# Layer 0: four of nine late output tiles as split products, and an earlier schedule for the modulation weights

## The chip, the cores and the metric

The kernel runs on one core of a Trainium2 chip. The metric is the device time of one execution in microseconds. TensorE (PE) multiplies, PEld is its loading of weights, VectorE (DVE) and ScalarE (ACT) work element by element, GpSimd (POOL) helps with a few additions, and SyncE (SP) issues nearly all transfers from HBM, in one queue and in the order of the program.

## The reference

Two layers of an encoder on 256 tokens of 2048 features, in float32. In each layer:

```
mod = silu(c) @ w_ada + b_ada            # six vectors of 2048: sh1, sc1, g1, sh2, sc2, g2
u = x*(1+sc1) + sh1;  proj = u @ w_in    # three head groups A (4), B (6), C (6 heads)
y = concat(rms_norm(A), rms_norm(B), rms_norm(C))
x = layer_norm(alpha*x + (1+g1) * (y @ w_o))
u = x*(1+sc2) + sh2;  h = silu(u@w_g) * (u@w_u)
x = layer_norm(alpha*x + (1+g2) * (h @ w_down))
```

## The kernel before, in words

Activations lie feature by feature: a tile is 128 features by 256 tokens, so 2048 features are 16 tiles (`KT`), and one output tile sums 16 products of a 128x128 weight with such a tile.

A product is made in one of two ways. **In float32** (`gemm_f32`, L277 to L283): each of the 16 products is one call, which stands in the trace as two matmul rows; the weights come as two transfers of 512 KB straight into one `hi` and one `lo` buffer (`wload_f32`), with no work on ACT or DVE. **Split** (`gemm_one`, `gemm_t`): a 1 MB transfer goes into a `raw` buffer; ACT rounds it to the high half (L254), DVE subtracts to get the low half (L255), both in two pieces of 1024 columns; then `gemm_one` runs three matmuls of 256 columns per product (high x high, high x low, low x high: L314 to L316). There are four `raw`, four `hi` and four `lo` buffers, taken in turn. The normalised head outputs are kept in both forms: `Yf` in float32, `Y` as high and low halves.

The modulation `mod` is made by DVE beside everything else. `ada(n)` takes the next of a list of 192 pieces: a 1 MB transfer of `w_ada` into a `raw` buffer (L205), and a multiply-and-sum on DVE (L207) at the lowest scheduling priority. Two things call it. `pace(us)` is called at each weight load (5.2 us' worth for 2048 columns) and each head (3.0) and adds `rate * us` to a credit; each whole unit of credit issues one piece. `need(l, part, k)` issues at once whatever is still missing of that part. The list runs, for layer 0: parts 1 and 0 (32 pieces, done with the first products), part 2 (16), parts 4 and 3 (32, the feed-forward's modulation), part 5 (16); then layer 1. `RATE[0][0]` is the rate from the end of the first input products to the late output tiles.

In layer 0 the order is: input products; norms of the latent vectors; head group A, then B, then C, each woven with products that fill TensorE (in C the first ten products of output tiles 0 to 6, split, from seven loads of `w_o`); the last six products of tiles 0 to 6; then the loop over the 16 output tiles in which tiles 7 to 15 are made whole (the nine late tiles). Each tile goes into the residual on DVE (L582) and its sums for the norm (L594, L597, L598). Tile 15 and the sums close the stage; the layer norm and the gate/up products follow, whose first tiles are a split stream of the `gemm_one` kind. In the loop, all `need` of part 2 is met; at tile 12 the missing pieces of parts 4 and 3 are issued and the rate is set to zero.

Of the kernel before, what the change touches and what calls it, by code (L numbers as in the profile page):

```python
# [21 lines left out]
KT = D // P  # L22
# [24 lines left out]
HO, KC = 7, 10  # L47
# [44 lines left out]
T2K, T1K, RAWB, HIB = 28, 31, 4, 4  # L92

DEFER = 4
RATE = ((0.24, 0.135, 0.135), (0.04, 0.05, 0.05))
NPOOL = 4


# [9 lines left out]
def tile_encoder(ctx: ExitStack, tc: tile.TileContext, xT, cB, w_ada, vecs, rpb, sink, consts,  # L108
# [24 lines left out]
    def pg(name):  # L133
        return ps.tile([P, 512], F32, tag="g", bufs=4, name=name)
# [80 lines left out]
    def need(l, part, k=KT - 1):  # L215
        g = ada_group(l, part)
        k += g - 1 - k % g
        while (l, part, k) in ada_pending:
            ada(1)
# [21 lines left out]
    def wload(src, cols, splits, gates=(), lo_eng=None):  # L241
        uid[0] += 1
        u = uid[0]
        pace(5.2 * cols / 2048)
        raw = wp.tile([P, 2048], F32, tag="raw", bufs=RAWB, name=f"raw{u}")
        sy.dma_start(out=raw[:, :cols], in_=src)
        res = []
        c0 = 0
        for i, n in enumerate(splits):
            hi = wp.tile([P, 1024], F32R, tag="hi", bufs=HIB, name=f"hi{u}_{i}")  # L250
            lo = wp.tile([P, 1024], F32R, tag="lo", bufs=HIB, name=f"lo{u}_{i}")
            eng = lo_eng[i] if lo_eng else ve
            with after(*gates):
                ac.activation(out=hi[:, :n], in_=raw[:, c0:c0 + n], func=AF.Copy)  # L254
                eng.tensor_tensor(out=lo[:, :n], in0=raw[:, c0:c0 + n], in1=hi[:, :n].bitcast(F32), op=ALU.subtract)  # L255
            res.append((c0, n, hi, lo))
            c0 += n

        def get(c, n):
            for s0, m, hi, lo in res:  # L260
                if s0 <= c and c + n <= s0 + m:
                    return hi[:, c - s0:c - s0 + n], lo[:, c - s0:c - s0 + n]
            raise AssertionError
        return get

    def wload_f32(src):

        uid[0] += 1
        pace(5.2)
        res = []  # L270
        for i, tag in enumerate(("hi", "lo")):
            w = wp.tile([P, 1024], F32, tag=tag, bufs=HIB, name=f"wf{uid[0]}_{i}")
            sy.dma_start(out=w, in_=src[:, i * 1024:(i + 1) * 1024])
            res.append(w)
        return res

    def gemm_f32(acc, w, X, kts, between=None):  # L277
        for i, k in enumerate(kts):
            if between and i == len(kts) - 4:
                between()  # L280
            m_ = pe.matmul(acc[:, :S], lhsT=w[i // 8][:, i % 8 * P:(i % 8 + 1) * P], rhs=X[k][:], start=(i == 0),  # L281
                           stop=(i == len(kts) - 1))
        last_mm[0] = raw_ins(m_)  # L283

    def gemm_t(acc, get, c0, X, kts):

        n = len(kts)
        for run in (range(n),):
            for i in run:
                pe.matmul(acc[:], lhsT=get(c0 + i * P, P)[0], rhs=X[kts[i]][:], start=(i == 0), stop=False)  # L290
            for i in run:
                last_mm[0] = raw_ins(pe.matmul(acc[:, :S], lhsT=get(c0 + i * P, P)[1], rhs=X[kts[i]][:, :S],  # L292
                                               start=False, stop=(i == n - 1)))

    def gemm_last(acc, get, X, kts, between=None):

        ops = []
        for i, k in enumerate(kts):
            h, lo = get(i * P, P)
            ops += [(h, X[k][:, :S]), (h, X[k][:, S:]), (lo, X[k][:, :S])]  # L300
        for i, (w, x) in enumerate(ops):
            if between and i == len(ops) - 12:
                between()
            m_ = pe.matmul(acc[:, :S], lhsT=w, rhs=x, start=(i == 0), stop=(i == len(ops) - 1))
        last_mm[0] = raw_ins(m_)

    def gemm_one(acc, get, c0, X, kts):

        for i, k in enumerate(kts):
            h, lo = get(c0 + i * P, P)  # L310
            mm_one(acc, h, lo, X[k], i == 0, i == len(kts) - 1)

    def mm_one(acc, h, lo, x, first, end, **kw):
        m_ = pe.matmul(acc[:, :S], lhsT=h, rhs=x[:, :S], start=first, stop=False, **kw)  # L314
        pe.matmul(acc[:, :S], lhsT=h, rhs=x[:, S:], start=False, stop=False, **kw)
        last_mm[0] = raw_ins(pe.matmul(acc[:, :S], lhsT=lo, rhs=x[:, :S], start=False, stop=end, **kw))  # L316
        return raw_ins(m_)
# [262 lines left out]
    def residual(l, acc, n, gate_, s1, s2, final, name, one=False):  # L580
        if final and (n == KT - 1 or one):
            ve.scalar_tensor_tensor(out=ax[:, n], in0=acc[:, :S], scalar=gate_, in1=ax[:, n], op0=ALU.mult, op1=ALU.add)  # L582
        else:
            t = tmp(f"rt_{name}")
            ac.activation(out=t, in_=acc[:, S:], func=AF.Identity, scale=gate_)  # L585
            (ve if final and n == KT - 2 else po).tensor_tensor(out=ax[:, n], in0=ax[:, n], in1=t, op=ALU.add)  # L586
            ve.scalar_tensor_tensor(out=ax[:, n], in0=acc[:, :S], scalar=gate_, in1=ax[:, n], op0=ALU.mult, op1=ALU.add)
        if final:
            if n == 0:
                ac.activation(out=s1, in_=ax[:, n], func=AF.Copy)  # L590
                ac.activation(out=s2, in_=ax[:, n], func=AF.Square)
            else:
                q = tmp(f"rq_{name}")
                i1 = ac.activation(out=q, in_=ax[:, n], func=AF.Square)  # L594
                if n == KT - 1:
                    return q
                (ve if one or n == KT - 2 else po).tensor_tensor(out=s1, in0=s1, in1=ax[:, n], op=ALU.add)  # L597
                d1 = ve.tensor_tensor(out=s2, in0=s2, in1=q, op=ALU.add)  # L598
                return raw_ins(d1), raw_ins(i1)
        return None  # L600

    allk = list(range(KT))
# [42 lines left out]
    def head_block(src, made, gates, name):  # L645
        accs = [pg(f"{name}_{i}") for i in range(4)] + [pa("s", 2, f"{name}_{i}") for i in range(4, HB)]
        st = Stream(_stream_head(), src, name, gates)
        for n, k in st.seq:
            st.load()
            if k not in X:  # L650
                X[k] = made(k)
            st.mm(accs[n], n, k, k == 0, k == KT - 1)
        return accs
# [3 lines left out]
    for l in range(L):  # L657
# [94 lines left out]
        if l == 0:  # L752
# [14 lines left out]
            def first_half(j):  # L767
                n = ROT[j]
                half = rot[:, j % 2 * S:(j % 2 + 1) * S]
                take(st_in.tile(n, 0, HK, half), dst[n][0], dst[n][1])  # L770
# [8 lines left out]
            first_half(HK)  # L779
            credit[1] = RATE[l][0]  # L780
            for n in RES[8:] + RES[:8]:
# [4 lines left out]
        else:  # L786
            sy.dma_start(out=nba, in_=rpb[l])
            X = {}
            accs = head_block(w_in[l], made, gates, f"in{l}")
            credit[1] = RATE[l][0]  # L790
            for n, acc in zip(HEAD1, accs):
# [7 lines left out]
        Y, Yf = [None] * KT, [None] * KT  # L799
# [150 lines left out]

        for n in range(KT):
            need(l, 2, KT - 1 if l else n)
            if n == KT - 4:
                need(l, 3, KT - 1 if l else KT - 1 - DEFER // 2)
                credit[1] = 0.0
            if n < HO:
                acc = oacc[n]
            else:
                acc = pg(f"o{l}_{n}")
                if l == 0:  # L960
                    gemm_f32(acc, wload_f32(w_o[l, n]), Yf, allk, sums_in if n == KT - 1 else None)
                else:
                    get = wload(w_o[l, n], 2048, (1024, 1024))
                    if n == KT - 1:
                        gemm_last(acc, get, Y, allk, sums_in)
                    else:
                        gemm_t(acc, get, 0, Y, allk)
            r_ = residual(l, acc, n, mods[l, 2][:, n:n + 1], s1, s2, True, f"o{l}_{n}", l == 0)
            if n == KT - 2:
                lastr = r_  # L970
# [26 lines left out]
        for g in range(FFG):  # L997
            credit[1] = RATE[l][1 if g == 0 else 2]
            H = []
            for j in range(GSZ):  # L1000
                f = g * GSZ + j
                hs = []
                for w in range(2):
# [5 lines left out]
                    if 2 * f + w < HB and l:  # L1009
                        acc = head[2 * f + w]  # L1010
                    else:
                        get = wload(w_gu[l, 2 * f + w], 2048, (1024, 1024))
                        acc = pg(f"gu{l}_{f}_{w}")
# [16 lines left out]
            c1 = (GSZ + 1) // 2  # L1030
            credit[1] = RATE[l][2]
            if g == FFG - 1:
# [5 lines left out]
            for n in range(KT):  # L1038
# [8 lines left out]
                get = wload(w_dn[l, g, n], GSZ * P, (c1 * P, (GSZ - c1) * P))  # L1047
                acc = pg(f"dn{l}_{g}_{n}")
# [137 lines left out]
```

## Time and profile before

| | |
|---|---|
| median of 3 runs | 2286.91 us (2285.03 to 2287.71) |
| the profiled execution | 2284.07 us |
| its span, first to last instruction | 2282.3 us |
| PE, PEld, DVE, ACT, POOL busy | 97%, 85%, 72%, 51%, 9% |
| mean rate of transfers over the span | 259 GB/s |

The late output tiles of layer 0 run from 360.4 to 424 us of the span, the three head groups from about 201 to 360 us. A group of the page gives busy time, the mean duration of one instruction, and the idle time of its engine just before; the chain of waits is followed back from the last instruction.

### The profile page before, as it was taken

The numbers are of one execution on the slowest core, as the hardware profiler recorded it, in microseconds if no ns is written. First come the engines' busy times: TensorE is split into PE (matmuls) and PEld (weight loads), VectorE is DVE, ScalarE is ACT, GpSimd is POOL, SyncE is SP. The second block draws the span as 40 slices with busy tenths as digits, with TensorE's granted clock in tenths as the row PEclk, the third lists the DMA queues.
The fourth block names the chain that finished last, engine by engine and source line by source line (L and its number), as shares of the span: only waits on it lengthen the run. The fifth ranks groups of instructions, "written<-read, shape, count | busy, mean of one in ns | idle before, by whom it ended". The sixth has DMA issues, their size and how long they took to land.

```text
span 2282.3 us, 32742 instructions
## 1 busy us (share of the span) xinstructions
PE 2224.7 (97%) x12670; PEld 1946.2 (85%) x12670; DVE 1654.6 (72%) x2340; ACT 1157.0 (51%) x1955; POOL 196.3 (9%) x169
## 2 busy tenths in 40 slices
PE   7989999999999999999999999989999999999997
PEld 5876888898888888888878888878888888888886
DVE  5537888688888888898887666788666665566566
ACT  1124562564554455445566566557454555445555
POOL 0000020000000200210320001320000020011014
PEclk9999999999999999999999999999999999999999
DMA  9987879478988899798756554456577566546543
GB/s 394 416 331 287 358 289 367 188 264 300 325 330 310 290 366 326 275 354 338 274 194 220 211 187 166 167 186 240 204 249 266 204 227 228 184 165 213 194 156 109
DMA packets 93902, 590.58 MB, mean 259 GB/s; under 512 B 10545, under 2 KB 10673, under 8 KB 39217
## 3 DMA queue, kind: packets, MB, share of 16 engines
q1 hardware_dynamic: 93746, 588.49, 70.1%
q8 instruction: 99, 1.62, 0.3%
q14 instruction: 57, 0.47, 0.1%
HBM read 586.35 MB, written 2.10 MB: 258 GB/s over the span
## 4 chain that ended last, share of the span: by engine, by line
PE 85%; DVE 5%; DMA 5%; ACT 2%; issue 1%; POOL 1%; ACTq 0%; DVEq 0%; SPq 0%
PE gu L290 25%; PE gu L292 13%; PE dn L290 13%; PE dn L292 7%; DMA ada<-in_w_ada 4%; PE o L281 3%; PE in L290 3%; DVE lo L255 2%; PE in L619 1%; DVE ada L207 1%; PE in_r L619 1%; PE in L292 1%; PE va L690 1%; PE oh L626 1%; ACT hi L254 1%
## 5 line engine op out<-in xcount | busy, mean ns | idle before, releaser
L255 DVE TENSOR_TENSOR lo<-raw,hi 128x1024 fp32r<-128x1024 f32 (+1 forms) x732 | 806.8, 1128 | 302.2 <-issue 138.8
L254 ACT ACTIVATE hi<-raw 128x1024 fp32r<-128x1024 f32 (+1 forms) x732 | 700.2, 961 | 446.5 <-PE gu L290 195.9
L290 PE MATMUL gu<-X,hi 128*128 128x512 f32 x2528 | 603.0, 391 | 0.0
L290 PEld LDWEIGHTS gu<-X,hi 128*128 128x128 f32 x2528 | 464.6, 188 | 89.9
L207 DVE CUSTOM_DVE_ANT_0 ada<-ada,cond,vec 128x2048 f32<-128x2048 f32 x192 | 452.3, 2358 | 96.5 <-DMA ada<-in_w_ada 86.3
L290 PE MATMUL dn<-H,hi 128*128 128x512 f32 x1386 | 339.7, 392 | 0.4 <-DVE H L341 0.4
L292 PEld LDWEIGHTS gu<-X,lo 128*128 128x128 f32 x2528 | 324.1, 191 | 12.3
L292 PE MATMUL gu<-X,lo 128*128 128x256 f32 x2528 | 328.0, 283 | 0.0
L290 PEld LDWEIGHTS dn<-H,hi 128*128 128x128 f32 x1386 | 252.4, 189 | 50.1 <-DVE H L341 3.2
L292 PEld LDWEIGHTS dn<-H,lo 128*128 128x128 f32 x1386 | 183.0, 191 | 9.9 <-DVE lo L255 0.3
L292 PE MATMUL dn<-H,lo 128*128 128x256 f32 x1386 | 186.4, 283 | 0.1
L336 POOL TENSOR_TENSOR mix<-mix,cma 128x256 f32<-128x256 f32 x64 | 78.5, 1227 | 1157.4 <-ACT cma L335 1115.5
L619 PE MATMUL in_r<-X,wf 128*128 128x256 f32 x448 | 103.9, 392 | 15.0 <-ACT X L442 15.0
L328 ACT ACTIVATE cmb<-gu 128x256 f32<-128x256 f32 x158 | 60.4, 382 | 108.5 <-PE gu L292 108.5
L619 PEld LDWEIGHTS in_r<-X,wf 128*128 128x128 f32 x448 | 87.4, 197 | 31.7 <-ACT X L442 19.3
L1020 ACT ACTIVATE gu<-gu 128x256 f32<-128x256 f32 x82 | 34.1, 417 | 84.0 <-DVE gu L331 83.9
L930 POOL TENSOR_SCALAR nbc<-cs 128x384 f32<-128x384 f32 x12 | 21.9, 1821 | 560.7 <-DVE mn_c L398 410.2
L290 PE MATMUL in<-X,hi 128*128 128x512 f32 x272 | 69.2, 401 | 0.0
L341 DVE TENSOR_TENSOR H<-gu,H 128x256 fp32r<-128x256 f32 x82 | 34.5, 423 | 46.0 <-ACT H L340 46.0
L331 DVE SCALAR_TENSOR_TENSOR gu<-gu,cmb 128x256 f32<-128x256 f32 x158 | 66.1, 419 | 0.5 <-ACT cmb L328 0.2
L290 PEld LDWEIGHTS in<-X,hi 128*128 128x128 f32 x272 | 49.8, 188 | 9.7
L586 POOL TENSOR_TENSOR ax<-ax,rt_dn 128x256 f32<-128x256 f32 x28 | 32.3, 1154 | 272.9 <-ACT rt_dn L585 272.9
(371 smaller groups left out, 2694.9 us busy)
## 6 DMA issues: line engine op xcount, KB each, us to landing
ada<-in_w_ada SPq DMA_DIRECT2D x192, 1024.0 KB, 6.6
raw<-in_w_gu SPq DMA_DIRECT2D x176, 1024.0 KB, 5.0
raw<-in_w_dn SPq DMA_DIRECT2D x128, 704.0 KB, 4.1
wf<-in_w_in SPq DMA_DIRECT2D x46, 512.0 KB, 11.9
raw<-in_w_o SPq DMA_DIRECT2D x23, 1024.0 KB, 4.8
raw<-in_w_in SPq DMA_DIRECT2D x23, 1024.0 KB, 4.8
wf<-in_w_o SPq DMA_DIRECT2D x18, 512.0 KB, 10.2
raw<-in_w_uq SPq DMA_DIRECT2D x6, 1024.0 KB, 4.8
```

Source lines behind the costliest of these rows:

```text
L207: ve.tensor_tensor_reduce(out=w, in0=w, in1=cond, op0=ALU.mult, op1=ALU.add, scale=1.0, scalar=vcol(l, V_ADA + part * KT + k), accum_out=m ...
L254: ac.activation(out=hi[:, :n], in_=raw[:, c0:c0 + n], func=AF.Copy)
L255: eng.tensor_tensor(out=lo[:, :n], in0=raw[:, c0:c0 + n], in1=hi[:, :n].bitcast(F32), op=ALU.subtract)
L281: m_ = pe.matmul(acc[:, :S], lhsT=w[i // 8][:, i % 8 * P:(i % 8 + 1) * P], rhs=X[k][:], start=(i == 0), stop=(i == len(kts) - 1))
L290: pe.matmul(acc[:], lhsT=get(c0 + i * P, P)[0], rhs=X[kts[i]][:], start=(i == 0), stop=False)
L292: last_mm[0] = raw_ins(pe.matmul(acc[:, :S], lhsT=get(c0 + i * P, P)[1], rhs=X[kts[i]][:, :S], start=False, stop=(i == n - 1)))
L328: ac.activation(out=t, in_=acc[:, S:], func=AF.Copy, scale=scale)
L331: ve.scalar_tensor_tensor(out=dst, in0=acc[:, :S], scalar=scale, in1=t, op0=ALU.mult, op1=ALU.add)
L336: po.tensor_tensor(out=dst, in0=dst, in1=t, op=ALU.add)
L341: return ve.tensor_tensor(out=dst[:, S:], in0=u, in1=dst[:, :S].bitcast(F32), op=ALU.subtract)
L619: last_mm[0] = raw_ins(pe.matmul(acc[:, :S], lhsT=w, rhs=X[k], start=first, stop=end, **kw))
L1020: silu[0] = raw_ins(ac.activation(out=hs[0], in_=hs[0], func=AF.Silu))
```

## The change

It makes late tiles 8, 10, 12 and 14 of layer 0 split products with `gemm_one` and `Y`; tiles 7, 9, 11, 13 and 15 stay in float32. It raises layer 0's first rate from 0.24 to 0.30 pieces per us of credit, and it asks for the feed-forward's modulation, and sets the rate to zero, at tile 7 where it was tile 12. Layer 1 keeps what it had.

```diff
-RATE = ((0.24, 0.135, 0.135), (0.04, 0.05, 0.05))
+RATE = ((0.3, 0.135, 0.135), (0.04, 0.05, 0.05))
...
         for n in range(KT):
             need(l, 2, KT - 1 if l else n)
-            if n == KT - 4:
+            if n == (HO if l == 0 else KT - 4):
                 need(l, 3, KT - 1 if l else KT - 1 - DEFER // 2)
                 credit[1] = 0.0
             if n < HO:
                 acc = oacc[n]
             else:
                 acc = pg(f"o{l}_{n}")
-                if l == 0:
+                if l == 0 and n % 2:
                     gemm_f32(acc, wload_f32(w_o[l, n]), Yf, allk, sums_in if n == KT - 1 else None)
                 else:
                     get = wload(w_o[l, n], 2048, (1024, 1024))
-                    if n == KT - 1:
+                    if l == 0:
+                        gemm_one(acc, get, 0, Y, allk)
+                    elif n == KT - 1:
                         gemm_last(acc, get, Y, allk, sums_in)
                     else:
                         gemm_t(acc, get, 0, Y, allk)
```

## Rows read from the trace of the kernel before

**Rows 1.** The page: busy time by engine, and the shares of the chain.
```profile
PE 2224.7 (97%) x12670; PEld 1946.2 (85%) x12670; DVE 1654.6 (72%) x2340; ACT 1157.0 (51%) x1955; POOL 196.3 (9%) x169
...
PE 85%; DVE 5%; DMA 5%; ACT 2%; issue 1%; POOL 1%; ACTq 0%; DVEq 0%; SPq 0%
```

**Rows 2.** Stretches, all engines: us, busy (x instructions) by engine, PEclk, DMA share, GB/s.
```profile
155.00:293.00 138.00, 133.59 (x651) 105.35 (x650) 95.35 (x157) 67.20 (x166) 0.00 (x0) 0.98 0.78 300
245.00:270.00 25.00, 25.00 (x154) 22.39 (x153) 22.92 (x34) 14.43 (x38) 0.00 (x0) 1.00 1.01 398
293.00:360.40 67.40, 63.86 (x450) 59.05 (x449) 66.10 (x127) 42.79 (x97) 12.91 (x6) 1.00 0.80 301
360.40:424.00 63.60, 63.07 (x297) 55.28 (x295) 38.98 (x65) 8.42 (x16) 0.00 (x0) 1.00 0.87 349
463.00:501.00 38.00, 38.00 (x319) 38.00 (x318) 32.10 (x44) 22.05 (x35) 0.00 (x0) 1.00 0.72 266
1397.00:1463.50 66.50, 65.90 (x398) 57.49 (x396) 48.06 (x114) 42.71 (x87) 8.45 (x6) 1.00 0.48 173
```

**Rows 3.** The chain of waits in order of time: start us, us, what.
```profile
303.29 2.00 DVE ada L207
309.09 1.13 DVE lo L255
...
360.42 60.44 PE o L281 x280
```

**Rows 4.** ScalarE's timeline in the late output tiles.
```profile
381.76 0.42 ACT L594 ACTIVATE rq_o<-ax 128x256 f32<-128x256 f32 x1 [6.49 <-DVE ax L582]
```

**Rows 5.** Stretches, line 207 alone (two instructions per reduction): DVE busy (x).
```profile
155.00:293.00 138.00, 58.53 (x50) 0.98 0.78 300
293.00:360.40 67.40, 31.07 (x26) 1.00 0.80 301
360.40:424.00 63.60, 21.11 (x18) 1.00 0.87 349
1397.00:1463.50 66.50, 4.71 (x4) 1.00 0.48 173
```

**Rows 6.** VectorE's timeline in the late output tiles: start us, us, instruction.
```profile
381.18 0.48 DVE L582 SCALAR_TENSOR_TENSOR ax<-o,mod,ax 128x256 f32<-128x256 f32 x1 [3.19 <-PE o L281]
...
388.09 0.48 DVE L582 SCALAR_TENSOR_TENSOR ax<-o,mod,ax 128x256 f32<-128x256 f32 x1 [3.18 <-PE o L281]
...
389.45 2.35 DVE L207 CUSTOM_DVE_ANT_0 ada<-ada,cond,vec 128x2048 f32<-128x2048 f32 x1
...
391.73 2.35 DVE L207 CUSTOM_DVE_ANT_0 ada<-ada,cond,vec 128x2048 f32<-128x2048 f32 x1
```

**Rows 7.** TensorE's timeline, split pieces of one gate/up tile.
```profile
463.00 0.28 PE L315 MATMUL gu<-X,hi 128*128 128x256 f32 x1
463.12 0.28 PE L316 MATMUL gu<-X,lo 128*128 128x256 f32 x1
463.24 0.28 PE L314 MATMUL gu<-X,hi 128*128 128x256 f32 x1
```

**Rows 8.** The page's groups: high and low halves of the weights.
```profile
L255 DVE TENSOR_TENSOR lo<-raw,hi 128x1024 fp32r<-128x1024 f32 (+1 forms) x732 | 806.8, 1128 | 302.2 <-issue 138.8
L254 ACT ACTIVATE hi<-raw 128x1024 fp32r<-128x1024 f32 (+1 forms) x732 | 700.2, 961 | 446.5 <-PE gu L290 195.9
```

**Rows 9.** Timelines of VectorE and TensorE at the end of head group C.
```profile
346.10 2.35 DVE L207 CUSTOM_DVE_ANT_0 ada<-ada,cond,vec 128x2048 f32<-128x2048 f32 x1
349.04 2.36 DVE L255 TENSOR_TENSOR lo<-raw,hi 128x1024 fp32r<-128x1024 f32 x2
...
350.32 1.10 PE L316 MATMUL oh<-Yc,lo 128*128 128x256 f32 x7 [1.39 <-DVE lo L255]
```

**Rows 10.** The DMA queue's timeline in the late output tiles.
```profile
370.41 14.85 SPq L205 DMA_DIRECT2D ada<-in_w_ada  x4
```

## The prediction

> **What bounds the kernel now.** I read the page first, then the chain of waits, then busy time by stretch, then the timelines of single engines. The page has TensorE busy 97% of the span and on 85% of the chain that ends last [rows 1]: the whole kernel is paced by it, and most transfers and casts hide behind it. The change touches two neighbouring stretches of layer 0, and they have different limits.
>
> The late output tiles (360.4 to 424 us) are TensorE alone: busy 63.07 of 63.60 us, VectorE 38.98, ScalarE 8.42 [rows 2], and the chain is one unbroken piece of 60.44 us [rows 3]. Per tile, ScalarE waits 6.49 us for the next result [rows 4]. Whatever shortens a tile here shortens the program.
>
> The head groups before (155 to 360 us) are close to two limits at once. In 293 to 360.4, head group C, TensorE is busy 63.86 of 67.40 us and VectorE 66.10 [rows 2]; 31.07 us of VectorE's time is the modulation's reduction, 26 rows, so 13 reductions [rows 5]. The chain there runs through VectorE, through that reduction and the low halves among others [rows 3]. So the part that the change makes denser lies where VectorE has 1.3 us free in 67.
>
> **The tiles.** The residual of one float32 tile follows that of the tile before by 388.09 - 381.18 = 6.91 us [rows 6]; no tile waits, so this is its cost. A split tile with this loop is 16 x 3 = 48 matmuls; in the gate/up tiles that are made the same way they start 0.12 us apart (463.00, 463.12, 463.24) [rows 7], and 319 fit in 38.00 us [rows 2], 0.119 each. 48 x 0.12 = 5.76 us. Four tiles: 4 x (6.91 - 5.76) = **4.6 us removed**, all on the chain.
>
> A page of the Trainium skill weighs this otherwise: "FP8 and Floating Point Precision", section TensorE Precision Notes, counts true float32 as four passes through the array, which against three split products would make a split tile three quarters of 6.91, 5.18 us, and four tiles 6.9 us shorter. The rows give 0.12 us a product, and I keep the measured 4.6.
>
> What the split tiles add beside it: per tile two high halves on ScalarE (0.96 us each) and two low halves on VectorE (1.13 us each) [rows 8]; four tiles, 7.7 us of ScalarE and 9.0 of VectorE. ScalarE has 55 us idle in the stretch. VectorE has 63.60 - 38.98 = 24.6 idle [rows 2], and nine reductions (18 rows, 21.11 us [rows 5]) that the earlier schedule takes away from there. So the casts cost nothing, as long as their weights are there; if that cover were gone, a late half would hold TensorE as it did in head group C, where a wait for one cost 1.39 us [rows 9]. The transfer is the same 1 MB in one issue for two. High buffers: a split tile takes two of four, and tile 10's second comes free in the middle of tile 8, one float32 tile and half a split tile (about 9.8 us) before it is needed, against some 4 us of casts. Tile 8 is the tight one: its cast falls among the seven residuals that VectorE does when the loop begins. I put 0.5 us on it (0 to 2.4, two low halves of 1.13 and a little).
>
> **The schedule.** I count the credit from the code. From where the rate starts to the beginning of head group C, loads and heads add up to 105.4 us of credit; C adds 44.0, the last two loads of the stream 10.4. At 0.24 this issues 25 pieces, then 10, then 3; the late tiles issue the remaining 10 of the 48 (six by rate, four at tile 12). At 0.30 it is 31, 13, 3, and one at tile 7. As a check, the trace of before has 25 reductions from 155 to 293 us, 13 from there to 360.4 and 9 behind (50, 26 and 18 rows [rows 5]): 47, and the one missing falls ahead of 155. So the change moves six reductions into the stretch before C, three into C, and takes nine from the late tiles. The total stays 48 at the same point, so the feed-forward starts with the same list.
>
> One reduction holds VectorE 391.73 - 389.45 = 2.28 us [rows 6].
>
> *Before C, six more:* 13.7 us of VectorE. In 155 to 293 it is idle for 138 - 95.35 = 42.7 us [rows 2], and TensorE has filler products there. Lower bound nothing, perhaps a little below, since the order on every engine is planned anew; upper bound two delays of a critical small operation by a whole reduction, 4.6 us. I take **+0.5**, near the lower end, because TensorE is busy 133.59 of 138 beside 25 reductions already.
>
> *In C, three more:* upper bound, all three inside the stretch and only 1.3 us free: 3 x 2.28 - 1.3 = 5.5 us. Lower bound from layer 1, whose same stretch (1397 to 1463.5) has two reductions [rows 5] and takes 66.50 us against 67.40 [rows 2]: eleven fewer bought 0.9 us, so three cost 0.25; and a different order could gain the 1.39 us that a reduction placed before two low halves cost at 350 us [rows 9]. In between: a reduction must be done only when its buffer is wanted by the load four further on. The last three or four pieces of the 48 hold buffers that tiles 10, 12 and 14 want, so they may be done behind 360.4, where VectorE is free; then C with its backlog does no more than the 13 it does now, only earlier in the list. Their low priority favours that; a plan whose durations differ from the chip's does not guarantee it. I take one more reduction inside the stretch, 2.28 - 1.3 = **+1.0 us**.
>
> *In the late tiles:* tile 12's four pieces now keep the queue for 14.85 us in the middle of the stage [rows 10], and TensorE doesn't notice. In the changed order tile 15's float32 load waits for a buffer of tile 12, and the feed-forward's first four `raw` loads queue behind it on SP. From there to the end of the stage are tiles 13 to 15, 6.9 + 5.8 + 6.9 = 19.6 us, and these 5 MB at 349 GB/s [rows 2] take 15. So the layer norm finds its first weights there, as now: 0, with 1.0 either way for the new order.
>
> **Sum:** -4.6 + 0.5 + 0.5 + 1.0 = **-2.6 us**. Against the profiled execution, 2284.07 (span 2282.3), that is 2281.5; the median of the runs shown, 2286.91, lies 2.8 us above that execution, so I forecast 2284.3.
>
> **Rivals.** What a measurement of this kernel can tell from no change is about 0.2%, 4.6 us: below 2282.3 counts as faster, above 2291.5 as slower.
>
> 1. *The cover holds everywhere.* The moved reductions are free: for it, VectorE's 42.7 idle us before C and layer 1's small difference; against it, 66.10 of 67.40 in C. The time is 2286.9 - 4.6 = 2282.3, and lower by up to 1.4 if the wait of [rows 9] goes too: 2280.9. Half of it counts as faster. Chance 0.35.
> 2. *VectorE becomes the bound of head group C* (slower). All three more reductions stay inside, because the loads of `w_o` wait for their buffers in turn: +5.5, with 0.5 before C and 0.5 at tile 8, net +1.9: 2288.8; one more wait like that of [rows 9] at each of two low halves makes it 2291.6. It decides from the second reduction that isn't put off: 1.3 us free, 2.28 each, so two cost 3.3 and, with the rest, eat the gain. For it: the chain runs through VectorE in C. Against: the buffers that allow putting off. Chance 0.18.
> 3. *Transfers become the bound of head group B.* In 245 to 270 the transfers take a share of 1.01 at 398 GB/s [rows 2]; three more pieces there at 1.049 MB / 398 GB/s = 2.63 us each would cost 7.9, net +3.8 or so: 2290.7. Against: the mean share before C is 0.78, and TensorE is busy all of those 25 us. The Trainium skill, "Perfetto Trace Analysis", section Roofline, puts the ceiling of one core's 16 DMA engines at about 435 GB/s, so by it little is left above 398 either, and the three would cost an estimated 7.2 us. Chance 0.05.
> 4. *The split tiles don't deliver.* Their weights come late tile after tile, and a split tile takes 6.9 us like the other: the 4.6 is gone, 2288.4. Against: 55 us of idle ScalarE. Chance 0.05.
>
> **How the numbers follow.** My forecast, a gain of 1 to 4 us (2283 to 2286), has 0.37. Its sum with the bounds: best 2280.9, worst 2291.6. The range 2281.0 to 2291.0 leaves out little but the ends of rivals 1 and 2. Faster by over 0.2%: half of rival 1 and a little of the forecast's edge, 0.22. Slower by over 0.2%: a third of rival 2, part of rival 3, 0.08. Within: 0.70.
>
> **What would show it.** In the changed kernel's trace: late residuals (L582) alternately 6.9 and 5.8 us apart and no TensorE idle at tile 8 (the tile step); 31 or 32 reductions done when C begins, 12 to 14 in C, up to four behind (the schedule); C's length, from the last values product to the first late tile, 67 to 69 us (the price), with TensorE waiting for low halves of `w_o` under 5 us. A C longer by 5 us, or residuals that are all 6.9 us apart, would prove the sum wrong, and so would a change outside 155 to 430 us of over 1 us, since nothing there should move.

## The result: slower by 13.3 us

The changed kernel takes 2299.31 us (median of 4 runs, 2298.70 to 2299.53) against 2285.97 (4 runs) for the kernel before: 1.0058 times as long, 95% interval 1.0046 to 1.0069. The forecast was 2284.3 with a range up to 2291.0, so the sign and the range were both wrong. The profiled execution took 2298.70 us, its span 2296.9; the page of the changed kernel hardly tells it from the one before [rows 1]:

```profile
PE 2225.5 (97%) x12734; PEld 1947.8 (85%) x12734; DVE 1664.8 (72%) x2348; ACT 1168.9 (51%) x1963; POOL 199.7 (9%) x169
...
PE 88%; DVE 4%; DMA 4%; ACT 2%; POOL 1%; issue 1%; SPq 0%; ACTq 0%; DVEq 0%
```

It has to be read by stage, and the stages move, so a fixed window no longer holds the same work. I cut at two marks on TensorE's timeline: the end of head group C's values products, and the first matmul of tile 7. Three stretches follow: from 201 us to the end of the values products ("A and B"), from there to tile 7 ("C"), and the late tiles. Those of the kernel before, with what lies ahead of them and the first part of A and B, by windows over all engines (columns as in [rows 2]):

```profile
155.00:201.00 46.00, 41.98 (x126) 24.38 (x125) 22.68 (x34) 12.69 (x34) 0.00 (x0) 0.93 0.64 234
...
201.00:299.90 98.90, 98.51 (x558) 87.05 (x557) 79.52 (x139) 59.01 (x142) 0.00 (x0) 1.00 0.81 317
299.90:360.30 60.40, 56.86 (x418) 52.88 (x417) 59.15 (x113) 38.29 (x89) 12.91 (x6) 1.00 0.86 323
360.30:423.50 63.20, 63.17 (x297) 55.38 (x296) 38.59 (x65) 8.42 (x16) 0.00 (x0) 1.00 0.87 349
...
201.00:245.00 44.00, 43.70 (x262) 39.08 (x261) 36.10 (x66) 29.76 (x69) 0.00 (x0) 1.00 0.78 298
```

and those of the changed kernel, with two windows inside A and B and one inside C:

```profile
201.00:308.20 107.20, 99.55 (x560) 87.55 (x559) 90.93 (x162) 62.53 (x153) 2.33 (x2) 1.00 0.87 345
308.20:381.00 72.80, 61.70 (x408) 55.67 (x407) 66.06 (x110) 35.36 (x76) 11.96 (x4) 0.88 0.86 323
381.00:439.60 58.60, 58.60 (x362) 54.11 (x360) 27.49 (x51) 16.72 (x25) 0.00 (x0) 1.00 0.57 218
...
201.00:245.00 44.00, 37.86 (x221) 33.38 (x220) 36.25 (x65) 25.51 (x61) 0.00 (x0) 1.00 0.86 333
245.00:293.00 48.00, 46.48 (x266) 40.72 (x266) 42.22 (x63) 27.39 (x68) 0.00 (x0) 1.00 0.97 388
330.00:360.00 30.00, 20.64 (x105) 17.49 (x103) 24.46 (x42) 13.86 (x32) 3.33 (x1) 0.72 0.79 298
```

A and B last 107.2 us instead of 98.9 with the same matmuls (560 and 558 rows): TensorE idles 7.65 us where it idled 0.39. Most of that, 6.14 us, lies from 201 to 245; only 1.52 lies from 245 to 293, where the transfers' share is highest. TensorE's waits in A and B are for high and low halves of the query weights, 4.5 us, and for small operations of the heads, 3.1 us. C lasts 72.8 instead of 60.4: TensorE idles 11.1 us instead of 3.5, and is busy 4.8 us longer at a granted clock of 0.88, the mean of stretches at its two levels. The late tiles last 58.6 instead of 63.2. Sum: 8.3 + 12.4 - 4.6 = 16.1, and -1.5 behind the late tiles makes the 14.6 by which the spans differ.

The late tiles do what was forecast. VectorE's timeline, residuals of tiles 7 to 10 [rows 6]:

```profile
388.81 0.47 DVE L582 SCALAR_TENSOR_TENSOR ax<-o,mod,ax 128x256 f32<-128x256 f32 x1
393.88 0.48 DVE L582 SCALAR_TENSOR_TENSOR ax<-o,mod,ax 128x256 f32<-128x256 f32 x1 [0.62 <-PE o L316]
400.79 0.48 DVE L582 SCALAR_TENSOR_TENSOR ax<-o,mod,ax 128x256 f32<-128x256 f32 x1 [5.51 <-PE o L281]
406.54 0.48 DVE L582 SCALAR_TENSOR_TENSOR ax<-o,mod,ax 128x256 f32<-128x256 f32 x1 [0.62 <-PE o L316]
```

400.79 to 406.54 is 5.75 us for a split tile, 393.88 to 400.79 is 6.91 for a float32 one, and TensorE is busy 58.60 of 58.60. The reductions moved as counted too. Line 207 alone, two rows for each [rows 5]:

```profile
155.00:308.20 153.20, 72.78 (x63) 0.99 0.79 307
308.20:381.00 72.80, 37.40 (x32) 0.88 0.86 323
381.00:440.00 59.00, 0.00 (x0) 1.00 0.57 219
```

By their starts 32, then 15, then none; by the same marks the kernel before had 26, 12 and 9. So the plan was carried out, and its price was wrong.

In C the loads of `w_o` go out late. The DMA queue's timeline before, from just ahead of C at 299.9:

```profile
299.13 0.33 SPq L246 DMA_DIRECT2D raw<-in_w_o  x1
302.94 6.14 SPq L205 DMA_DIRECT2D ada<-in_w_ada  x3
311.51 0.33 SPq L246 DMA_DIRECT2D raw<-in_w_o  x1
314.56 2.96 SPq L205 DMA_DIRECT2D ada<-in_w_ada  x2
321.16 0.33 SPq L246 DMA_DIRECT2D raw<-in_w_o  x1
```

and after, C from 308.2:

```profile
313.64 0.33 SPq L246 DMA_DIRECT2D raw<-in_w_o  x1
316.86 10.07 SPq L205 DMA_DIRECT2D ada<-in_w_ada  x4
328.87 0.33 SPq L246 DMA_DIRECT2D raw<-in_w_o  x1
331.73 6.66 SPq L205 DMA_DIRECT2D ada<-in_w_ada  x3
344.68 0.33 SPq L246 DMA_DIRECT2D raw<-in_w_o  x1
```

The second, third and fourth load, 10 to 12 us apart with three and two pieces between them, became loads 15 to 16 us apart with four and three. The first, 279.15 before, now went out at 297.89, and the seven take 69.3 us to go out where they took 62.1. The high halves follow them late too. ScalarE's timeline before, the first one, ahead of C:

```profile
296.07 1.04 ACT L254 ACTIVATE hi<-raw 128x1024 fp32r<-128x1024 f32 x1
```

and after, the first, 5 us into C, and the third with what stands ahead of it:

```profile
313.38 1.99 ACT L254 ACTIVATE hi<-raw 128x1024 fp32r<-128x1024 f32 x2
...
340.93 0.38 ACT L815 ACTIVATE yrc<-yc 128x256 f32<-128x256 f32 x1 [2.17 <-PE yc L423]
341.21 1.99 ACT L254 ACTIVATE hi<-raw 128x1024 fp32r<-128x1024 f32 x2
```

That third cast belongs to the load of 328.87. In ScalarE's order it stands behind a head's operation, which waits for TensorE. The weights were there: from 290 to 350 the loads of `w_o` land 4.7 to 6.6 us after their issue (where the trace has the landing), this one by 335.5 at the latest, and ScalarE sat idle for 2.17 us just before the operation at 340.93. The fourth cast, at 354.40, likewise comes at least 3 us after its load of 344.68 has landed, behind an operation of the heads' norm that waits 2.88 us for VectorE. Only the sixth, at 366.83, waits for its transfer, 4.86 us. And TensorE, with no products of `w_o` left to fill in, first walks through the heads' steps bare and then waits for the casts, the third and the fourth (TensorE's timeline, after):

```profile
342.31 0.58 PE L314 MATMUL oh<-Ya,hi 128*128 128x256 f32 x1 [1.42 <-ACT hi L254]
355.50 0.58 PE L314 MATMUL oh<-Yb,hi 128*128 128x256 f32 x1 [3.34 <-ACT hi L254]
```

Of TensorE's 11.1 us of idle time in C, 5.4 are waits for high halves, 0.4 for low halves and some 5 for the heads' small operations.

What the idle costs a second time, windows of 5 us over all engines:

```profile
330.00:335.00 5.00, 2.65 (x18) 2.06 (x16) 5.00 (x11) 3.60 (x12) 2.45 (x1) 1.00 1.02 408
335.00:340.00 5.00, 3.44 (x11) 2.19 (x12) 3.45 (x9) 2.17 (x6) 0.88 (x1) 0.65 0.87 311
340.00:345.00 5.00, 3.43 (x13) 2.42 (x12) 2.71 (x4) 3.86 (x5) 0.00 (x0) 0.50 0.43 179
345.00:350.00 5.00, 5.00 (x37) 5.00 (x37) 4.53 (x4) 0.00 (x0) 0.00 (x0) 0.82 0.82 300
```

TensorE idles from 330, and the clock goes from 1.00 to 0.50, that is from 2.4 to 1.2 GHz; at 345 it has work again and the clock still averages 0.82.

### The profile page after: what moved, and what is told of

The parts are those of the page before. It is cut to its first block, busy times and chain, and to the rows that moved or that the text cites. A ratio compares the mean times of both kernels' runs of the same rounds, so it can differ in the third digit from the quotient of the medians.

```text
span 2296.9 us, 32870 instructions
## 1 busy us (share of the span) xinstructions
PE 2225.5 (97%) x12734; PEld 1947.8 (85%) x12734; DVE 1664.8 (72%) x2348; ACT 1168.9 (51%) x1963; POOL 199.7 (9%) x169
## 4 chain that ended last, share of the span: by engine, by line
PE 88%; DVE 4%; DMA 4%; ACT 2%; POOL 1%; issue 1%; SPq 0%; ACTq 0%; DVEq 0%
PE gu L290 25%; PE dn L290 14%; PE gu L292 13%; PE dn L292 7%; DMA ada<-in_w_ada 3%; PE in L290 3%; DVE ada L207 2%; PE o L281 2%; PE in L292 1%; PE in_r L619 1%; PE in L619 1%; DVE lo L255 1%; PE va L690 1%; PE oh L626 1%; PE gu_h L626 1%; PE in L626 1%
## 5 line engine op out<-in xcount | busy, mean ns | idle before, releaser
L255 DVE TENSOR_TENSOR lo<-raw,hi 128x1024 fp32r<-128x1024 f32 (+1 forms) x740 | 819.4, 1134 | 312.7 <-issue 142.7
L254 ACT ACTIVATE hi<-raw 128x1024 fp32r<-128x1024 f32 (+1 forms) x740 | 709.8, 963 | 446.5 <-PE gu L290 193.1
```

## The experiments

Times are medians against the kernel before, run on the same chip, with the ratio's 95% interval. Behind each stand the lengths of A and B, C, and the late tiles in its profiled execution, by the marks above: 98.9 / 60.4 / 63.2 before, 107.2 / 72.8 / 58.6 after.

### The parts alone

The rate alone, on the kernel before:

```diff
-RATE = ((0.24, 0.135, 0.135), (0.04, 0.05, 0.05))
+RATE = ((0.3, 0.135, 0.135), (0.04, 0.05, 0.05))
```

> Only the first rate of layer 0 goes from 0.24 to 0.30; late tiles stay float32, tile 12 still asks for what is missing. Theory 1 (the queue): the denser pieces stand in the transfer queue, in order, in front of the head groups' weights and hold the four raw buffers, TensorE runs out of products in head group C and its clock falls; the loss is the rate's alone and the split tiles give back 4.6 us, so this kernel is slower than the changed one: +16 to +20 us over before, 2302 to 2306. Theory 2 (VectorE's time): nine reductions of 2.28 us come into head groups, +20 us at most less what is idle, +5 to +20. Theory 3 (the split tiles' casts and loads disturb the plan): about 0, within 2 us of before.

2308.72 against 2286.38, 1.0092 (1.0076 to 1.0108): +22.3. 107.9 / 71.8 / 63.3. The head groups' whole loss is the rate's.

The four split tiles alone (`if l == 0 and n % 2` and the `gemm_one` branch):

> Only the four split tiles; rate 0.24 and the request at tile 12 as before. Theories 1 and 2: the head groups are as before and the late tiles give 4.6 us; six pieces by rate now share the raw buffers with the split tiles, which may cost 0 to 3: 2281 to 2285, 1 to 4.6 below before. Theory 3: +10 us or more.

2290.01, 1.0019 (1.0010 to 1.0028): +3.6 where a gain was expected. 98.6 / 60.4 / 70.0: the head groups are those of before, but the late tiles take longer than in float32. DMA queue's timeline:

```profile
375.52 11.05 SPq L205 DMA_DIRECT2D ada<-in_w_ada  x4
391.10 2.60 SPq L246 DMA_DIRECT2D raw<-in_w_o  x2
```

With the old schedule the split tiles' loads take `raw` buffers in turn with the pieces and stand behind four of them; TensorE then waits 4.5 us for a high half, from 394, and 4.1 us in two waits for low halves. A float32 tile uses no `raw` buffer. So here the split tiles pay only where no pieces stand beside them.

The early request alone, and with the split tiles, both at 0.24:

```diff
-            if n == KT - 4:
+            if n == (HO if l == 0 else KT - 4):
```

> Only the request for the feed-forward's modulation at tile 7 (rate 0.24, late tiles float32): ten pieces stand in the queue in front of tile 7's weights. Theory 1 (queue and buffers): a piece takes a raw buffer until it is reduced, so ten pieces take at least 10 x 2.5 us before tile 7's transfers can be issued; the stream's last products cover about 9 us of it, so TensorE stands 10 to 25 us: 2296 to 2311. Theory 2 (VectorE's time): VectorE has 24.6 us idle in the late tiles and the pieces are merely earlier in them: 0, 2285 to 2288.

> Split tiles and the early request, rate 0.24. Theory 1: as the early request alone less 4.6 us at most: 2292 to 2307. Theory 2: -4.6, 2280 to 2284. If it is the plan's order that decides and no sum, this is more than 4 us off the sum of the two single edits.

Request alone: 2304.51, 1.0078 (1.0063 to 1.0093), +18.1; 97.5 / 66.8 / 76.5. With the split tiles: 2300.40, 1.0066 (1.0048 to 1.0085), +14.0; 98.7 / 66.8 / 75.5. The pieces asked for at tile 7 hold up the tiles' own weights: in the request alone TensorE waits 15.3 us for them. So the nine or ten pieces cost 18 to 22 us wherever they are put ahead of tile 7, in one heap or by the rate, and the parts don't add: in the change the rate has already issued all but one. Splitting then gives back 9 of the 22.3 in the medians, and 4.7 in the late tiles (63.3 to 58.6); the other four are not explained, the rate's own four runs being spread over 9 us.

Half of the rate's step (0.27, 43 pieces ahead of tile 7 by the credit, for 38 and 47):

> The kernel before with the first rate at 0.27 alone (float32 tiles, request at tile 12): 28 pieces before head group C for 25 and 31, half of the step to 0.30, which cost 22 us. Either theory with a threshold at the full transfer engines or full buffers: between before and 0.30, 2290 to 2302, and less than half of the 22 if there is slack at first. If it is the plan's order that scatters by itself: anything, perhaps below before.

2297.36 against 2286.04, 1.0044 (1.0028 to 1.0059): +11.3. 102.9 / 70.7 / 63.3. By the credit this is three more pieces for the 4.0 us in A and B, and 1.3 more for the 10.3 us in C. The trace counts otherwise: 28 reductions start from 155 us to the end of the values products, where the kernel before has 26 and the changed one 32, and 15 start in C, as many as in the changed kernel. So A and B pay 1.4 to 2.0 us for each reduction more, and C has nearly its whole price at half of the step in the rate, with as many pieces worked off in it; whether C's price goes in a step or by the piece isn't shown.

### Which resource

Reductions of parts 2 to 5 over half of their columns, transfers whole; and both halved. These leave out half of that modulation's sums.

```diff
+                cw = D // 2 if l == 0 and part >= 2 else D
-                ve.tensor_tensor_reduce(out=w, in0=w, in1=cond, ...
+                ve.tensor_tensor_reduce(out=w[:, :cw], in0=w[:, :cw], in1=cond[:, :cw], ...
...
-            sy.dma_start(out=w, in_=w_ada[l, part * KT + k])
+            sy.dma_start(out=w[:, :cw], in_=w_ada[l, part * KT + k][:, :cw])
```

> The changed kernel with layer 0's parts 2 to 5 reduced over half of each piece only (1.14 us of VectorE for 2.28; the transfer stays 1 MB, the other half is left out of the sum). Theory 2 (VectorE's time): the denser pieces then take less of VectorE than before's did, so the split tiles' gain shows: 2279 to 2284. Theory 1 (buffers and queue): a piece now holds its raw buffer some 10 us from issue to reduction plus the reduction; that falls by 1.1 of 12 to 13, a tenth, and VectorE comes to the next one sooner: 2288 to 2297.

> As the half reduction, with the transfer halved too (512 KB of each of those pieces; half of the sum left out). Theory of the transfers' rate: 24 MB fewer in the head groups, the loss goes: 2279 to 2284, and the half reduction alone stays near 2299. Theory 1 (buffers and queue): a piece lands 2 to 3 us earlier, so another fifth of its hold goes: 2284 to 2293. Theory 2: as the half reduction, no further gain over 2 us.

VectorE relieved alone: 2298.30 against 2286.93, 1.0047 (1.0032 to 1.0062): +11.4 where the change has +13.3, its own interval reaching from 10.5 to 15.8. The transfer halved too: 2276.76, 0.9957 (0.9942 to 0.9972): all 13 us back and 10 more. Of the ten, 4.6 are the late tiles' own gain and 4.1 come from A and B (97.8) and C (57.4), shorter than in the kernel before. The first two stretches, reductions halved:

```profile
201.00:311.60 110.60, 102.75 (x559) 90.08 (x558) 68.35 (x165) 63.06 (x155) 3.44 (x2) 0.97 0.84 331
311.60:379.20 67.60, 58.09 (x410) 53.37 (x408) 48.91 (x108) 35.35 (x76) 6.75 (x4) 0.95 0.90 344
```

and both halved:

```profile
201.00:298.80 97.80, 97.41 (x556) 86.55 (x555) 70.76 (x159) 60.45 (x143) 0.00 (x0) 1.00 0.80 287
298.80:356.20 57.40, 55.88 (x417) 52.84 (x416) 40.70 (x105) 40.33 (x91) 10.91 (x6) 1.00 0.59 211
```

With VectorE idle for 42 of 110.6 us, A and B are as slow as ever, even 3.4 us slower; in C, where VectorE idles 18.7 us, 5.2 of the 12.4 us come back. That is about what can be VectorE's there; the edit also frees each buffer sooner and has the order of all engines planned anew. With the bytes halved too the loss is gone.

The same relief given to the transfer engines elsewhere: the head groups' ten float32 weight tiles loaded by half, 5.2 MB less, pieces and reductions as in the change. It leaves out the other half of those weights.

```diff
+        n_ = 512 if credit[1] else 1024
-            sy.dma_start(out=w, in_=src[:, i * 1024:(i + 1) * 1024])
+            sy.dma_start(out=w[:, :n_], in_=src[:, i * 1024:i * 1024 + n_])
```

> The changed kernel with the float32 weights of the head groups (ten tiles: values of A and C and the last input products, 10 MB) loaded by half, 5 MB, and that half used twice (the other half is left out); pieces, raw buffers and reductions are as in the changed kernel. Theory D (transfer rate): 5 MB less is like five pieces less of the nine, over half of the loss goes: 2284 to 2291. Theory B (buffers' turn): these weights don't lie in raw buffers, little changes: 2295 to 2300.

2287.95 against 2286.04, 1.0010 (1.0001 to 1.0019): 11.4 us of the 13.3 are back, 9.5 of them in A and B, which is 1.8 us for each MB.

```profile
201.00:298.70 97.70, 96.76 (x551) 85.61 (x550) 86.32 (x146) 56.93 (x139) 0.00 (x0) 1.00 0.89 340
298.70:371.80 73.10, 62.40 (x417) 57.03 (x416) 66.61 (x120) 42.01 (x91) 18.11 (x6) 0.93 0.82 308
```

A and B are cured (97.7) although VectorE does all its reductions (86.32 busy), so there it is the bytes in transit. From 201 to 245 TensorE now idles 0.9 us (6.1 in the change). Which transfer delays which wait isn't traced: in the change TensorE's waits in A and B are for split weights and small operations, none for a float32 weight. C is as long as in the change (73.1), but none of the halved loads falls into it. So this run shows that C's loss isn't handed on from A and B; it doesn't show that C's own transfers are free. Note that the share of the transfer engines in A and B doesn't fall, it is 0.89.

For C, two tries at how the pieces stand in the way. Pieces issued from GpSimd's queue, so that no load stands behind one in SP's:

```diff
-            sy.dma_start(out=w, in_=w_ada[l, part * KT + k])
+            (po if l == 0 and part >= 2 else sy).dma_start(out=w, in_=w_ada[l, part * KT + k])
```

> The changed kernel with the pieces of layer 0's parts 2 to 5 issued from GpSimd's queue, the weights still from SyncE's. Buffers are taken in the same turn. Theory 1a (the queue's order is what holds the weights): a piece that waits for its buffer no longer keeps the loads behind it, most of the loss goes: 2281 to 2288. Theory 1b (the four buffers are what holds them): a weight load still waits for its own buffer, held by a piece: 2294 to 2302. GpSimd's own additions in the feed-forward wait behind its transfers, which may cost 0 to 5 either way.

2303.48 against 2286.93, 1.0074 (1.0059 to 1.0089). 113.2 / 68.3 / 58.6: C gets 4.5 us back, and A and B lose 6.0 more. Taking the pieces out of the weights' queue is no cure.

Pieces of parts 2 to 4 in two 512 KB buffers of their own, in halves, and three `raw` buffers for the rest:

```diff
-T2K, T1K, RAWB, HIB = 28, 31, 4, 4
+T2K, T1K, RAWB, HIB = 28, 31, 3, 4
...
+                    w = wp.tile([P, D // 2], F32, tag="ada", bufs=2, name=f"ada{l}_{part}_{k}_{h}")
```

> The changed kernel with layer 0's parts 2 to 4 in two buffers of their own of 512 KB (each piece as two half transfers and two half reductions, the second added to the first), and three raw buffers for the weights instead of four; one queue. Theory 1b (buffers): the weights no longer wait for pieces to be reduced, the head groups return to within 5 us of before: last late tile ends at 420 to 428 us of the span for 439.7. Theory 1a (queue order): the pieces still wait in the queue, with fewer bytes of buffer, and the weights behind them: last late tile at 437 to 450. The three raw buffers can cost the rest of the kernel something, so the stage is compared and not the total.

2334.98, 1.0218 (1.0188 to 1.0247): the third `raw` buffer is missed all through the feed-forward. But the stages of interest:

```profile
201.00:309.50 108.50, 99.26 (x558) 86.74 (x557) 75.36 (x160) 62.53 (x143) 0.00 (x0) 1.00 0.80 283
309.50:369.40 59.90, 56.94 (x418) 53.10 (x416) 46.39 (x114) 38.79 (x87) 8.93 (x6) 1.00 0.72 247
```

C is 59.9, as long as before. That speaks for the shared buffers in C. But three of its loads of `w_o` had gone out by 247 us, 62 us ahead of C, with fewer pieces in flight the transfer share in C is lower as well (0.72), and A and B have their own trouble with three buffers.

Reductions of parts 2 to 4 at high priority, so that buffers come free sooner:

```diff
-            with after(gate[0]), tc.high_priority(100 if l == 0 and part < 2 else -1000):
+            with after(gate[0]), tc.high_priority(100 if l == 0 and part < 5 else -1000):
```

> The changed kernel with all of layer 0's reductions of parts 2 to 4 planned at high priority, so that a piece is reduced when it has landed: same bytes, same VectorE time, a raw buffer held some 4 us less of 12 to 13. Theory B (the four buffers' turn): the weights behind them come sooner, 2285 to 2293. Theory D (the transfer engines' rate, 16 engines near their full share in head group B): no gain, 2295 to 2302; or a loss, as critical small operations of VectorE now wait for 2.28 us each.

2305.24 against 2286.04, 1.0083 (1.0070 to 1.0097). 106.4 / 83.0 / 58.6: C loses ten more. TensorE waits 6.7 us for one low half there. So reducing the pieces sooner doesn't cure C; as these reductions now stand ahead of other work on VectorE, the run doesn't rule out the buffers either.

Over the runs with whole pieces, wholly reduced, in SP's queue and four buffers, C's length goes with the number of reductions that start in it: 57.9 to 60.4 us with 12, 64.6 to 66.8 with 13, 70.7 to 73.1 with 15 or 16, and 83.0 with 15 at high priority. A longer stage also leaves time for more of them, so this alone doesn't say which makes which.

### Is there room earlier?

From 155 to 201 us transfers had a share of 0.64 before the change. So: the changed kernel with a rate of 0.60 over the loads there, then 0.25; and the kernel before with 0.45, then 0.209, alone and with tiles 13 and 14 split.

```diff
+        if l == 0:
+            credit[1] = 0.25
         fc = [w_in_(n) for n in (14, 15, 8, 9, 10, 11, 12, 13)]
```

> The changed kernel with the same 48 pieces by tile 7 but placed otherwise: rate 0.60 over the four value loads of group A (12 pieces for 6), then 0.25 through head groups A to C (about as many there as in the kernel before). Theory (place, not number): the stretch 155 to 201 us has transfers at a share of 0.64 and no weights in raw buffers, so the early pieces are nearly free and the head groups run as before; the late tiles keep their 4.6: first late tile at 358 to 363 us of the span, last ends at 416 to 422, in all 2278 to 2284. If it is the number of pieces ahead of tile 7 that costs, wherever they stand: still 2294 or more.

> The kernel before with the rate 0.45 over the same four loads, then 0.209: 38 pieces ahead of tile 7 as before, four fewer of them in head groups A to C. If a piece in the head groups costs its 2.3 us in the kernel before too, -6 to -9: 2277 to 2280. If 0.24 lies under the threshold, as its TensorE waits of about 9 us from 200 to 360 us say at most: -1 to -4, 2282 to 2285. By number alone: 0.

> The early pieces and the two last split tiles together: the sum of both, that of the two tiles having been -5.5 by the timed runs and -2.4 by the profile: 2276 to 2282, below both kernels.

Against 2286.47: the changed kernel so 2300.40, 1.0059 (1.0047 to 1.0071), no better than without; the kernel before 2291.92, 1.0021 (1.0012 to 1.0029), +5.4 where a gain was expected (the waits of about 9 us that its forecast names are 3.9 by the marks); with two split tiles 2286.35, 0.9999 (0.9990 to 1.0007). Placed like this, the pieces find no free room there. In the first of them, the DMA queue's timeline:

```profile
176.81 0.86 SPq L273 DMA_DIRECT2D wf<-in_w_va  x2
181.23 13.95 SPq L205 DMA_DIRECT2D ada<-in_w_ada  x3
195.27 0.86 SPq L273 DMA_DIRECT2D wf<-in_w_va  x2
```

Group A's value weights wait behind three pieces for 14 us, and A and B take 114.4 us (105.4 in the second). C gets shorter (64.6 here, 57.9 in the second, with fewer pieces in it), so the price moves with the pieces and doesn't vanish.

### A version that beats both

The kernel before, unchanged schedule, with the two tiles split that come behind the last pieces:

```diff
-                if l == 0:
+                if l == 0 and n not in (13, 14):
...
+                    if l == 0:
+                        gemm_one(acc, get, 0, Y, allk)
```

> The kernel before with two split tiles only, 13 and 14, behind the last pieces of w_ada; rate and request as before. Every theory that puts the loss on pieces standing with weights: the two tiles have no piece beside them, 2 x 1.15 = 2.3 us less: 2283.5 to 2286, ratio 0.999. If the split tiles themselves or the feed-forward's first loads behind them disturb the end of the stage: 2288 or more.

2280.55 (10 runs) against 2286.04 (20 runs), 0.9977 (0.9968 to 0.9986): 5.5 us faster than the kernel before and some 19 faster than the changed one.

```profile
358.90:420.40 61.50, 61.18 (x330) 54.83 (x328) 42.92 (x69) 12.33 (x20) 0.00 (x0) 1.00 0.92 358
```

The late tiles are 1.7 us shorter (two split tiles would give 2 x 1.15 = 2.3), the span of the profiled execution 2.4 (2279.9 for 2282.3). The medians say more, 5.5 and at least 3.2 by the interval. Single executions differ by as much: the profiled one of the kernel before lies 2.0 us below the median of its 20 runs, that of this kernel 1.3 above its own, so the traces can't place the rest.

## Why the prediction was wrong

**The tiles: right.** -4.6 forecast, 63.2 - 58.6 = 4.6 measured; a split tile 5.76 forecast, 5.75 measured, and tile 8's 0.5 was 0. The Trainium skill's count of four passes for float32 ("FP8 and Floating Point Precision", TensorE Precision Notes), by which a split tile would have been an estimated 5.18 us, doesn't agree with the 5.75 and 6.91 here. But "the casts cost nothing, as long as their weights are there" held only since the schedule was empty by then; with pieces beside them the same tiles cost 3.6 us more than float32.

**The counts: right to one.** 31 or 32, 12 to 14 and up to four reductions were forecast by stage; 32, 15 and none came, in C one more than forecast. The putting off of three or four past C, on which my +1.0 rested, did not happen: all three more stayed inside.

**The schedule's price: the step that failed.** "Before C, six more: +0.5" measured 8.3, "in C, three more: +1.0" measured 12.4. Both lie beyond the upper bounds of 4.6 and 5.5, because both were worked out in VectorE's time, 2.28 us a reduction. The bytes that a piece moves, the buffer that it holds and what it does to the order of the other engines' work stood in the sum at nothing. The halved reductions show that A and B don't pay in VectorE's time at all (0 of 8.3 us back) and C at most in part (5.2 of 12.4); the halved float32 loads show that A and B pay in bytes. Nine or ten more pieces ahead of tile 7 cost 22.3 and 18.1 us, 1.8 to 2.5 each, against 1.049 MB / 388 GB/s = 2.7 for the transfer alone.

*A and B* are rival 3's mechanism, to which I gave 0.05, in another place. It named head group B by the row of 245 to 270 at a share of 1.01 [rows 2]. TensorE's idle time lies ahead of that, from 201 to 245; there, too, the kernel before had the transfers at a share of 1.00 from 201 to 207, and of 0.78 in the mean. I set the mean share of 0.78 and a TensorE busy in all 25 us against it. Neither speaks: the mean holds stretches that the pieces could not use (the experiments on an earlier place), and a TensorE that is busy now doesn't say that the weights two stages on are in time. I also gave the rival three pieces in one group; there were six over both. The Trainium skill's ceiling of some 435 GB/s ("Perfetto Trace Analysis", Roofline) is not reached in any window shown here: the fullest have 388 GB/s over 48 us, at a share of 0.97, and 408 over 5 us.

*C* is rival 2's place, and its mechanism only in part. Its condition held (three more reductions inside, VectorE's busy time up from 59.15 to 66.06), and its 5.5 us is close to what halving the reductions gave back, 5.2. But VectorE's idle time in C rose as well, from 1.3 to 6.7 us, and the wait that it names, for low halves, is 0.4 us. The other 7 us, and all of the 12.4 with pieces halved or in their own buffers, went away when the pieces took fewer bytes or other buffers. What the trace shows of the way there: the loads of `w_o` go out later, the first cast comes 9 us later in C (5 us into it, where it was 4 us ahead) and the first product 5.8 us later (314.49, or 6.3 us into C, for 300.43, or 0.5), the heads' steps lie bare, casts stand behind them on ScalarE although their weights have landed, and the clock falls. Part of it was readable before: [rows 9] has TensorE waiting for a half of `w_o` already, and in the queue one to three pieces stood between two such loads. What in C does most is not told apart and stays open: the shared buffers, the transfers, or the order that the planner gives the casts among the heads' operations. Own buffers came with half pieces and fewer in flight, high priority made it worse, and a fifth `raw` buffer or casts moved ahead of the heads' operations were not tried.

**Nothing outside 155 to 430 should move by over 1 us:** behind the late tiles the changed kernel is 1.5 us shorter, 1857.3 us for 1858.8. In the profiled executions of the other kernels with four `raw` buffers that rest lasts 1854.9 to 1860.4 us, so a difference of 1.5 tells nothing. And C's length, which I put at 67.4 before, is 60.4 by the mark that I named; my window began 7 us early, in the values products.

## What to carry to other kernels

A background stream is priced in every resource that it takes (engine time, bytes, buffers, a place in the queue and in the order of each engine), and by the windows of a stage, not by its mean; a busy TensorE says nothing of the slack of the loads behind it. Moving such work earlier to clear one stage puts it in front of another's weights: find out first what the receiving stage pays for one piece more. A tile form that takes from a shared ring of buffers is cheap only where the ring's other user is done, which is why two split tiles at the end beat four spread over the stage with a new schedule.

## What was unexpected of the hardware

From 330 to 360, where TensorE was busy for 20.64 of 30 us, the granted clock was 0.72 on average and 0.50 from 340 to 345, and the waits so cost more than their length: in C TensorE's busy time went from 56.86 to 61.70 us with ten matmul rows fewer. The transfer engines gave 388 GB/s over 48 us at a share of 0.97, and taking 5.2 MB of other loads off them gave back 1.8 us per MB in A and B, where this rate makes 2.6 us of a MB.
